# A hybrid mixer block: the gate logits of gated linear attention as a task of their own

## The chip, the cores and the metric

One core of one Trainium2 chip runs the whole block. The time is the device time of one execution in microseconds (us); of the kernel before, three runs gave 1382.53, 1382.78 and 1385.5, with the median 1382.78. Its five engines are TensorE (PE in the rows; PEld is its loading of weights), VectorE (DVE), ScalarE (ACT), GpSimd (POOL) and SyncE (SP, which issues most DMAs).

## The reference, cut to what matters

Two layers, each with four branches on the same normalised input: latent attention (MLA), neighbourhood attention, Hyena convolution, gated linear attention (GLA). There are 256 latent tokens and 256 context tokens; layer 0 gives out both streams, layer 1 only the latent one. The branches' outputs are gated, projected, weighted by merge gates and summed. What the change touches is the decay of GLA:

```python
def feats(hh):
    q, k = jnp.split(in_proj(hh, w_in, 'gla_qk').astype(f32), 2, axis=-1)
    ...
    glr = in_proj(hh, w_in, 'gla_glr').astype(f32).reshape(B, L, 2, GLA_GATE_RANK)
    logit = jnp.einsum('blir,ire->blie', glr, wg2.astype(f32)) + bg.astype(f32)
    log_a = (jax.nn.log_sigmoid(logit) / GLA_TAU).reshape(B, L, 2, GLA_HEADS, GLA_DK)
    return q, k, v, log_a

def gla_chunked(q, k, v, log_a, s0):
    ...
    b = jnp.cumsum(g, axis=3)          # g: log_a in chunks of 64 tokens
    a = jnp.einsum('nbhtd,nbhsd->nbhts', q * jnp.exp(b - b_mid), k * jnp.exp(b_mid - b))
    ...
```

The logarithm of the sigmoid is written as min(x, 0) - ln(1 + exp(-|x|)), where x is the logit with its bias. It is needed for all 512 tokens in two directions, 256 channels each: four tiles of 128 x 512 per layer.

## The kernel before, in words

Nearly all products are made of three passes (mm3): each operand is split into a rounded high part and a rest, and high x high, high x low and low x high are summed in PSUM. For weights, the method piece loads 512 KB into one of three raw buffers through SyncE's queue, ScalarE casts the high part (wh, line 439) and VectorE subtracts (wl, line 380). Names in the rows: pc and pj are projections by channel and by token, br the branch projection into the merged sum, sc the scores, pt the transposed probabilities, y the attention's output, lg the gate logits, ktp the transposed keys of GLA, kv, atp and go its state, score and output products, ot the transposes of its output.

The order of TensorE's instructions is written out by hand. Generators ("tasks") yield either a delay or a condition. The driver has a clock of its own, which each product moves on by a cost; it takes the first task by priority whose delay is over, and so lays out one fixed queue for TensorE. Priority 0 goes first (attention units, GLA's passes), then 1 (MLA, GLA), 2 (the adaLN weights), and 5, the main line with the projections, fills what is left. The delays stand in the table WAIT, a pair for each name, for layer 0 and layer 1. They only decide where on TensorE's queue a product stands; the hardware waits by semaphores. The order on the other engines is chosen by a planner from the program's order and modelled times, and tiles get free buffers of their pool there. Pools that matter: T (15 buffers of 128 x 512), S (20), G (8, which the merge gates and filters use), raw (3).

The main line of a layer: MLA's gate, then gla_in (queries, keys and values of GLA), while MLA runs as a task; the merge gates of branch 0, first half; a wait for MLA's end; branch 0's projection, first half; then the GLA task starts (method gla). Beside it run the second half of branch 0's merge gate and projection, GLA's gate gla_z, and both halves of the merge gate of branch 3; then the main line waits for GLA's end and projects it.

GLA itself first loads the logits' weights (raw, wg), splits them, makes the four logit tiles in PSUM (lg), and computes on VectorE mn = min(x, 0), ee = max(x, 0), ee = mn - ee, which is -|x|. ScalarE then takes Exp and Ln of the four tiles in this order (line 1196), and GpSimd subtracts. Then come two passes over pairs of heads, each with two directions (gla_dir): a scan over the decays on VectorE (line 1238), exponentials, the transposes ktp, the states, scores and outputs. The second pass starts when the first has ended. At last come a norm and the transposes ot.

Of the kernel before, what the change touches and what calls it, by code (L numbers as in the profile page):

```python
# [12 lines left out]
AF = mybir.ActivationFunctionType  # L13
ALU = mybir.AluOpType
# [111 lines left out]
def _layout(x, c, ctx, c_ctx, ada_w, ada_b, pre_g, post_g, w_in, mla_q_norm, mla_w_uq, mla_kv_norm, mla_w_ukv, na_rpb,  # L126
# [78 lines left out]


WAIT = {
    "ada_at0": (6.0, 8.0),
    "ada_at1": (6.0, 11.0),
    "ada_at2": (15.0, 17.0),  # L210
    "ada_at3": (17.5, 19.5),
# [3 lines left out]
    "norm": (4.23, 4.0),  # L215
    "norm_turn": (5.27, 5.25),
    "norm_ab": (0.16, 0.69),
    "norm_step": (1.25, 0.52),
    "filt_in": (3.1, 4.0),
    "filt_sin1": (6.0, 15.54),  # L220
    "filt_sin2": (6.0, 4.8),
# [2 lines left out]
    "filt_sum": (10.0, 11.8),  # L224
    "filt_norm": (7.2, 15.6),
    "filt_dft": (0.3, 0.5),
    "filt_out": (1.82, 4.9),
    "probs": (5.63, 6.08),
    "probs2": (7.2, 7.6),
    "probs_out": (1.36, 1.35),  # L230
    "values_out": (1.14, 5.3),
    "latent_in": (1.5, 1.5),
    "latents": (10.0, 12.0),
    "latents_out": (5.62, 0.49),
    "mla_keys": (1.6, 1.78),
    "mla_v": (0.32, 0.22),
    "mla_k": (0.8, 2.25),
    "mla_q": (0.08, 0.5),
    "mla_q_out": (1.7, 1.04),
    "na_in": (2.87, 0.97),  # L240
    "hy_turn": (2.18, 3.82),
    "hy_turn_step": (0.35, 0.5),
    "hy_turn_out": (0.5, 0.67),
    "hy_dft": (1.57, 1.8),
    "hy_product": (13.35, 11.95),
    "hy_mid": (0.35, 0.81),
    "hy_out_step": (0.72, 0.5),
    "hy_order": (6.38, 0.9),
    "hy_out": (1.3, 1.0),
    "gla_in": (2.65, 0.53),  # L250
    "gla_logit": (2.0, 0.1),
    "gla_decay": (7.1, 2.9),
    "gla_dir": (6.79, 4.0),
    "gla_norm": (14.0, 4.73),
    "gla_turn": (0.03, 0.45),
    "gla_out": (1.66, 1.98),
    "gla_keys": (6.49, 5.03),
    "gla_kT": (0.9, 1.07),
    "gla_at": (0.5, 0.5),
    "gla_scores": (6.1, 4.0),  # L260
    "gla_o": (2.0, 1.09),
    "merged": (4.6, 3.55),
    "merged_step": (0.48, 0),
    "merged_out": (1.6, 1.24),
    "norm_first": (3.27, 8.0),
}

# [6 lines left out]
class Block:  # L274
# [890 lines left out]
        v = yield from self.tok_values(l, "gla_v")  # L1165
        return q, k, v

    def gla(self, l, outs, qkv, g, ys):
        nc, d = self.nc, self.d
        q, k, v = qkv  # L1170
        lo = outs[0] * 256
        raw = self.T("wg2", (P, 2, 2, P))
        nc.gpsimd.dma_start(raw[:96], d["wg2"][l])
        wg = self.tp.tile([P, 2, 2, P], F32R, tag="t", name=self.name("wg"))
        nc.scalar.copy(wg[:96], raw[:96])
        self.sub(nc.vector, wg[32:64], raw[32:64], wg[32:64].bitcast(F32))
        yield self.wait("gla_in")
        la, es = {}, {}
        for p in range(2):
            for r in range(2):  # L1180
                ps = self.ps(self.pa, "lg")

                self.mm(ps, wg[:96, r, p, :], self.glrT[:96, :])
                mn, mx = self.S("mn"), self.T("ee")
                bg = self.pp(l, "bg", 2 * r + p)
                self.ts(mn, ps, bg, ALU.add, 0.0, ALU.min)
                self.ts(mx, ps, bg, ALU.add, 0.0, ALU.max)
                self.sub(nc.vector, mx, mn, mx)
                la[p, r], es[p, r] = mn, mx
                yield self.wait("gla_logit")  # L1190

        last = None
        for f, bias in ((AF.Exp, 0.0), (AF.Ln, 1.0)):
            for e in es.values():
                with self.tc.issue_after(last) if last is not None else nullcontext():
                    i = nc.scalar.activation(e, e, f, bias=bias)
                last = i.ins if hasattr(i, "ins") else i
        for key, e in es.items():
            self.sub(nc.gpsimd, la[key], la[key], e)
        yield self.wait("gla_decay")  # L1200
        o = [self.S("glao", (P, 4, P)) for _ in range(4)]
        for p in range(2):
            ts_ = []
            for r in range(2):
                ts_.append(self.spawn(self.gla_dir(p, r, outs, la[p, r], q[p], k[p], v, o), 0))
                yield self.wait("gla_dir")
            yield lambda: all(t.done for t in ts_)
        t0 = 2 * outs[0]
        nt = 4 - t0
        ss = []  # L1210
        for h in range(4):
            sq = self.T("osq", (P, 4, P))
            ss.append(self.t(4, "oss"))
            nc.scalar.activation(sq[:, t0:], o[h][:, t0:], AF.Square)
            nc.vector.tensor_reduce(out=ss[h][:, :nt], in_=sq[:, t0:], axis=AX.X, op=ALU.add)
        for h in range(4):
            rs = self.rstd(ss[h][:, :nt], nt, 1.0 / P)
            self.mul(nc.vector, o[h][:, t0:], o[h][:, t0:], rs.unsqueeze(2).to_broadcast([P, nt, P]))
        yield self.wait("gla_norm")
        yield lambda: g() is not None  # L1220
        for h in range(4):
            ps = self.ps(self.pt, "ot")
            for tt in range(t0, 4):
                self.tr(ps[:, tt * P : tt * P + P], o[h][:, tt, :])
            y = self.T("y32")
            self.stt(y[:, lo:], ps[:, lo:], self.pp(l, "gla_norm"), g()[h][:, lo:], ALU.mult, ALU.mult)
            self.split(ys[0][h][:, lo:], ys[1][h][:, lo:], y[:, lo:], nc.gpsimd)
            yield self.wait("gla_turn")
        yield self.wait("gla_out")
# [187 lines left out]
    def layer(self, l, ws):  # L1417
        nc, d = self.nc, self.d
        self.l = l
        outs = (0, 1) if l < DEPTH - 1 else (1,)  # L1420
# [5 lines left out]
        lats = []  # L1426
# [10 lines left out]
        gz = {}  # L1437
        ys = self.ytiles()
# [5 lines left out]
        mla = self.spawn(start_mla(), 1)  # L1444
        gz["mla"] = yield from self.zgate(l, "mla_z", outs, True)
        qkv = yield from self.gla_in(l, outs)
        if l == 0:
            self.rest = self.spawn(self.ada_rest(), 2)
        gates = yield from self.gate_list(l, 0, (0,), outs)
# [4 lines left out]
                merged[s, half] = self.M("merged")  # L1454
        box = {}
        yield from self.merge_list(l, 0, (0,), gates, ys, merged, True)
        gla = self.spawn(self.gla(l, outs, qkv, lambda: gz.get("gla"), box), 1)
        gates = yield from self.gate_list(l, 0, (1,), outs)
        yield from self.merge_list(l, 0, (1,), gates, ys, merged, True)
        ys = self.ytiles()  # L1460
# [126 lines left out]
```

## Time and profile before

| | us |
|---|---|
| median of the runs | 1382.78 |
| profiled execution, its own time | 1384.55 |
| its span, first to last instruction | 1382.8 |
| TensorE busy | 1311.0 |
| VectorE busy | 898.5 |
| ScalarE busy | 604.2 |
| GpSimd busy | 319.1 |

The profile comes from one execution. Busy times are of instructions that work, not of waits. A product's start and end are modelled, so products that follow one another overlap in the rows. In a row of waits, "PE ktp <- DVE ktl" is idle time of TensorE ahead of ktp that ended when VectorE had written ktl. The granted clock is a share of full speed, 2.4 GHz; at 0.5 TensorE runs at 1.2 GHz. "issue" means that no releaser shows.

### The profile page before, as it was taken

What the parts mean: (1) busy time and instruction counts of PE and PEld (TensorE: products, weight loads), DVE (VectorE), ACT (ScalarE), POOL (GpSimd) and SP (SyncE); (2) the same over time, 40 slices, a digit from 0 to 9 for tenths busy, and PEclk for the clock granted to TensorE, in tenths of its full rate; (3) what the DMA queues carried; (4) which work ended last, traced back from release to release, by engine and by line L of the source; (5) the groups of instructions that cost most, each with busy time, mean ns of one, the idle gap of its engine ahead of it and who ended that gap; (6) DMA issues with size and microseconds to landing.
All of it is one profiled execution on the core that took longest, in us unless ns stands there. A gap on an engine that the chain in (4) does not pass through costs nothing.

```text
span 1382.8 us, 20166 instructions
## 1 busy us (share of the span) xinstructions
PE 1311.0 (95%) x7444; PEld 1033.8 (75%) x7444; DVE 898.5 (65%) x1676; ACT 604.2 (44%) x1268; POOL 319.1 (23%) x408
## 2 busy tenths in 40 slices
PE   6999999989999999999999999989996999999997
PEld 3877677767877776766767777778775899788875
DVE  5678663675443446556566587887677787768763
ACT  4555553432323233222344543565546456444552
POOL 2332201243320101123201122442104331122110
PEclk9999999999999999999999999999998999999998
DMA  9521223332243433423422343433143366435361
GB/s 349 204 92 39 91 77 97 101 99 78 92 125 135 141 118 109 135 92 106 139 92 81 103 153 111 158 107 114 42 147 92 108 198 210 157 108 166 109 217 56
DMA packets 55506, 171.07 MB, mean 124 GB/s; under 512 B 7470, under 2 KB 10128, under 8 KB 55408
## 3 DMA queue, kind: packets, MB, share of 16 engines
q1 hardware_dynamic: 49056, 153.31, 33.6%
q0 software_dynamic: 5440, 16.16, 3.6%
q8 instruction: 59, 0.97, 0.3%
q10 hardware_dynamic: 912, 0.31, 0.1%
q14 instruction: 39, 0.32, 0.1%
HBM read 163.45 MB, written 6.31 MB: 123 GB/s over the span
## 4 chain that ended last, share of the span: by engine, by line
PE 42%; DVE 7%; issue 3%; ACT 2%; DMA 2%; POOL 1%; DVEq 0%; POOLq 0%; ACTq 0%
PE pc L390 12%; PE pj L390 11%; PE br L390 5%; PE wo L390 3%; PE sc L390 2%; PE y L390 2%; PE pt L404 2%; DVE wl L380 2%; PE pa L390 1%; PE yc L390 1%; ACT wh L439 1%; DMA raw<-in_w_out 1%; DMA raw<-in_w_in 1%; DVE ub L374 0%; DVE wr L380 0%
## 5 line engine op out<-in xcount | busy, mean ns | idle before, releaser
L380 DVE TENSOR_TENSOR wl<-raw,wh 128x512 fp32r<-128x512 f32 (+1 forms) x416 | 300.3, 744 | 178.1 <-ACT wh L439 175.8
L439 ACT CAST wh<-raw 128x512 fp32r<-128x512 f32 (+1 forms) x416 | 248.5, 618 | 273.1 <-DMA raw<-in_w_in 143.4
L390 PE MATMUL pc<-hh,wh 128*128 128x256 f32 (+1 forms) x688 | 242.4, 352 | 6.5 <-DVE xt L387 2.7
L390 PE MATMUL pc<-hh,wl 128*128 128x256 f32 (+1 forms) x688 | 231.4, 336 | 0.0
L390 PE MATMUL pc<-hl,wh 128*128 128x256 f32 (+1 forms) x688 | 230.9, 336 | 0.0
L390 PE MATMUL pj<-wh,hh 128*128 128x512 f32 x512 | 213.2, 416 | 2.8 <-ACT wh L439 1.8
L390 PE MATMUL pj<-wl,hh 128*128 128x512 f32 x512 | 200.4, 391 | 0.4 <-DVE wl L380 0.4
L390 PE MATMUL pj<-wh,hl 128*128 128x512 f32 x512 | 200.3, 391 | 0.0
L390 PEld LDWEIGHTS pc<-hh,wh 128*128 128x128 f32 x688 | 132.1, 192 | 32.1 <-issue 15.1
L390 PEld LDWEIGHTS pc<-hl,wh 128*128 128x128 f32 x688 | 132.2, 192 | 14.3 <-issue 2.6
L390 PEld LDWEIGHTS pc<-hh,wl 128*128 128x128 f32 x688 | 131.8, 192 | 13.6
L390 PEld LDWEIGHTS pj<-wh,hh 128*128 128x128 f32 x512 | 96.4, 188 | 33.1 <-issue 12.4
L390 PEld LDWEIGHTS pj<-wh,hl 128*128 128x128 f32 x512 | 96.2, 188 | 21.1
L390 PEld LDWEIGHTS pj<-wl,hh 128*128 128x128 f32 x512 | 96.6, 189 | 20.3 <-issue 2.6
L380 POOL TENSOR_TENSOR gl<-y,gh 128x256 fp32r<-128x256 f32 (+1 forms) x44 | 36.2, 829 | 295.0 <-ACT gh L422 295.0
L826 ACT ACTIVATE p<-sc,mx 128x512 f32<-128x512 f32 (+1 forms) x96 | 58.9, 615 | 59.4 <-DVE mx L824 56.2
L390 PE MATMUL br<-wh,gh 128*128 128x512 f32 x192 | 79.2, 412 | 4.8 <-DVE merged L383 2.8
L390 PE MATMUL br<-wl,gh 128*128 128x512 f32 x192 | 76.9, 400 | 0.0
L390 PE MATMUL br<-wh,gl 128*128 128x512 f32 x192 | 76.7, 399 | 0.1
L1340 ACT ACTIVATE gt<-pj 128x512 f32<-128x512 f32 x48 | 28.6, 596 | 91.0 <-PE pj L390 88.5
L824 DVE TENSOR_REDUCE mx<-sc 128x1 f32<-128x512 f32 (+1 forms) x96 | 55.0, 591 | 11.4 <-PE sc L390 10.5
L841 ACT COPY pt<-pt 128x256 f32<-128x256 f32 x96 | 34.2, 372 | 43.1 <-PE pt L404 42.1
(287 smaller groups left out, 2227.0 us busy)
## 6 DMA issues: line engine op xcount, KB each, us to landing
raw<-in_w_in SPq DMA_DIRECT2D x160, 512.0 KB, 3.6
adaw<-in_ada_w SPq DMA_DIRECT2D x36, 512.0 KB, 3.6
raw<-in_w_branch SPq DMA_DIRECT2D x32, 512.0 KB, 3.7
raw<-in_w_out SPq DMA_DIRECT2D x16, 512.0 KB, 4.3
adaw<-in_ada_w SPq DMA_DIRECT2D x24, 256.0 KB, 5.2
H<-filt POOLq DMA_DIRECT2D x16, 256.0 KB, 4.3
nab<-in_na_bias POOLq DMA_DIRECT2D x16, 256.0 KB, 3.1
raw<-in_w_in SPq DMA_DIRECT2D x8, 448.0 KB, 4.5
```

The lines of the kernel that those rows point to most:

```text
L380: eng.tensor_tensor(out=out, in0=a, in1=b, op=ALU.subtract)
L390: self.nc.tensor.matmul(out, lhsT, rhs, start=start, stop=stop, skip_group_check=skip)
L404: self.nc.tensor.transpose(out, in_, self.ident)
L439: nc.scalar.copy(hi, raw[:, sl])
L824: nc.vector.tensor_reduce(out=mx, in_=ps[h][:, :nk], axis=AX.X, op=ALU.max, negate=True)
L826: nc.scalar.activation(p[h][:, :nk], ps[h][:, :nk], AF.Exp, bias=mx, scale=1.0, accum_out=sm)
L841: nc.scalar.copy(pts[h][b // 2], pp[:, b : b + 2, :])
L1340: self.nc.scalar.activation(gates[s, t], ps, AF.Tanh, scale=0.5)
```

## The change

The first half of gla becomes a method and task of its own, gla_logits, which the layer starts with priority 1 as soon as gla_in has ended (and the four latent tasks, which make glrT, are done; they are by then). gla starts where it did, waits for that task on the driver's clock, and goes straight to its passes. In the logits' work, VectorE keeps the min; ScalarE writes the absolute value from PSUM with the bias added, and Exp takes the sign by its scale, so the max and the difference go. mn moves from pool S to pool G. Eighteen entries of WAIT change; those of the two stages here are shown.

```diff
-    "ada_at0": (6.0, 8.0),
+    "ada_at0": (3.68, 7.47),
-    "probs_out": (1.36, 1.35),
+    "probs_out": (1.36, 0.94),
-    "mla_v": (0.32, 0.22),
+    "mla_v": (0.32, 0),
-    "mla_q": (0.08, 0.5),
+    "mla_q": (0.15, 0),
-    "hy_turn": (2.18, 3.82),
+    "hy_turn": (1.49, 4.79),
-    "gla_in": (2.65, 0.53),
-    "gla_logit": (2.0, 0.1),
+    "gla_in": (2.65, 0.67),
+    "gla_logit": (1.02, 0.1),
-    "gla_dir": (6.79, 4.0),
+    "gla_dir": (6.31, 4.0),
-    "gla_scores": (6.1, 4.0),
-    "gla_o": (2.0, 1.09),
+    "gla_scores": (5.09, 7.57),
+    "gla_o": (2.0, 1.05),
...
-    def gla(self, l, outs, qkv, g, ys):
+    def gla_logits(self, l, lats, la):
+
         nc, d = self.nc, self.d
-        q, k, v = qkv
-        lo = outs[0] * 256
+        yield lambda: len(lats) == 4 and all(t.done for t in lats)
         raw = self.T("wg2", (P, 2, 2, P))
         nc.gpsimd.dma_start(raw[:96], d["wg2"][l])
...
-        la, es = {}, {}
+        es = {}
...
-                mn, mx = self.S("mn"), self.T("ee")
+                mn, ab = self.G("mn"), self.T("ee")
                 bg = self.pp(l, "bg", 2 * r + p)
+                nc.scalar.activation(ab, ps, AF.Abs, bias=bg)
                 self.ts(mn, ps, bg, ALU.add, 0.0, ALU.min)
-                self.ts(mx, ps, bg, ALU.add, 0.0, ALU.max)
-                self.sub(nc.vector, mx, mn, mx)
-                la[p, r], es[p, r] = mn, mx
+                la[p, r], es[p, r] = mn, ab
                 yield self.wait("gla_logit")
...
-        for f, bias in ((AF.Exp, 0.0), (AF.Ln, 1.0)):
+        for f, scale, bias in ((AF.Exp, -1.0, 0.0), (AF.Ln, 1.0, 1.0)):
...
+    def gla(self, l, outs, qkv, la, logits, g, ys):
+        nc = self.nc
+        q, k, v = qkv
+        lo = outs[0] * 256
+        yield lambda: logits.done
...
         qkv = yield from self.gla_in(l, outs)
+        la = {}
+        logits = self.spawn(self.gla_logits(l, lats, la), 1)
```

## Rows read from the trace of the kernel before

**Rows 1.** the page's first part: busy us, share of the span, instructions
```profile
PE 1311.0 (95%) x7444; PEld 1033.8 (75%) x7444; DVE 898.5 (65%) x1676; ACT 604.2 (44%) x1268; POOL 319.1 (23%) x408
```

**Rows 2.** stretches: us, busy us (count) PE, PEld, DVE, ACT, POOL, clock, DMA, GB/s
```profile
1008.00:1029.50 21.50, 21.39 (x108) 16.29 (x106) 12.72 (x24) 12.10 (x25) 1.77 (x3) 1.00 0.40 132
1029.50:1113.66 84.16, 71.53 (x566) 60.12 (x565) 67.26 (x132) 44.30 (x85) 33.11 (x54) 0.92 0.34 107
1043.60:1053.90 10.30, 0.00 (x0) 0.00 (x0) 5.64 (x6) 8.83 (x13) 7.74 (x7) 0.75 0.48 150
1053.90:1062.70 8.80, 7.83 (x58) 6.37 (x59) 6.24 (x13) 2.13 (x5) 1.60 (x5) 0.51 0.05 20
203.00:246.00 43.00, 43.00 (x222) 31.89 (x221) 19.41 (x41) 16.33 (x35) 3.51 (x6) 1.00 0.35 114
```

**Rows 3.** TensorE's waits, 1000 to 1130: total us, times, longest
```profile
PE ktp L404 <- DVE ktl L374: 10.3, 1, 10.3
```

**Rows 4.** timeline, layer 1's GLA: start us, us, instruction, idle before
```profile
1030.86 0.40 PE L390 MATMUL lg<-glrT,wg 96*128 96x512 f32 x1
1045.52 2.27 DVE L1238 TENSOR_TENSOR_SCAN gb<-scan_mask,mn 128x512 f32<-128x512 f32 x1 [1.98 <-POOL mn L380]
1053.92 1.11 PE L404 MATMUL ktp<-ident,ktl 128*128 128x128 f32 x4 [10.33 <-DVE ktl L374]
1058.54 1.82 PE L390 MATMUL kv<-gla_v,kT 64*64 64x128 f32 x20 [0.95 <-ACT kT L1263]
1110.52 0.38 PE L404 MATMUL ot<-ident,glao 128*128 128x128 f32 x2
```

**Rows 5.** timeline of ScalarE there, its table loads
```profile
1042.22 1.28 ACT L1196 ACT_TABLE_LOAD   x1
1045.20 1.28 ACT L1340 ACT_TABLE_LOAD   x1
1047.11 1.28 ACT L1196 ACT_TABLE_LOAD   x1
1050.08 1.28 ACT L1250 ACT_TABLE_LOAD   x1
```

**Rows 6.** tiles mn, ee, wg: ns min/median/max, first and last start
```profile
L387 DVE TENSOR_SCALAR mn<-lg,par x8: 739/746/752, 250.0 to 1036.7; 128x512 f32<-128x512 f32 x8
L387 DVE TENSOR_SCALAR ee<-lg,par x8: 739/740/743, 250.7 to 1037.4; 128x512 f32<-128x512 f32 x8
L380 DVE TENSOR_TENSOR ee<-mn,ee x8: 677/682/693, 251.5 to 1039.8; 128x512 f32<-128x512 f32 x8
L1196 ACT ACTIVATE ee<-ee x16: 612/630/634, 252.2 to 1048.4; 128x512 f32<-128x512 f32 x16
L380 POOL TENSOR_TENSOR mn<-mn,ee x8: 1262/1291/2179, 264.0 to 1049.1; 128x512 f32<-128x512 f32 x8
L1175 ACT CAST wg<-wg x2: 609/616/622, 227.5 to 1028.2; 96x512 fp32r<-96x512 f32 x2
DMA to landing us min/median/max: 2.7/2.8/2.9
```

**Rows 7.** timeline: issues of the logits' weights; MLA's last value product
```profile
212.53 0.54 POOL L1173 DMA_DIRECT2D wg<-in_wg  x1
1008.50 0.54 POOL L1173 DMA_DIRECT2D wg<-in_wg  x1
1021.32 1.95 PE L390 MATMUL y<-pt,mlav 128*64 128x256 f32 x16
```

**Rows 8.** TensorE's waits from 250 to 345, layer 0's GLA
```profile
PE ada L390 <- issue: 4.9, 2, 3.7
PE br L390 <- DVE merged L383: 2.8, 1, 2.8
PE ktp L404 <- DVE ut L383: 0.9, 1, 0.9
```

**Rows 9.** groups of ScalarE: busy, mean ns, idle before
```profile
L754 ACT ACTIVATE fabs<-filt 128x512 f32<-128x512 f32 x16 | 9.8, 627 | 7.3 <-DVE filt L374 7.2
```

More of the change, by code (lines that the diff above doesn't have):

```diff
@@ L217 @@
     "norm_ab": (0.16, 0.69),
-    "norm_step": (1.25, 0.52),
+    "norm_step": (0.65, 0.52),
     "filt_in": (3.1, 4.0),
@@ L226 @@
     "filt_dft": (0.3, 0.5),
-    "filt_out": (1.82, 4.9),
+    "filt_out": (1.82, 4.04),
     "probs": (5.63, 6.08),
-    "probs2": (7.2, 7.6),
-    "probs_out": (1.36, 1.35),
+    "probs2": (7.2, 7.7),
+    "probs_out": (1.36, 0.94),
     "values_out": (1.14, 5.3),
-    "latent_in": (1.5, 1.5),
+    "latent_in": (2.81, 1.5),
     "latents": (10.0, 12.0),
@@ L235 @@
     "mla_keys": (1.6, 1.78),
-    "mla_v": (0.32, 0.22),
+    "mla_v": (0.32, 0),
     "mla_k": (0.8, 2.25),
-    "mla_q": (0.08, 0.5),
+    "mla_q": (0.15, 0),
     "mla_q_out": (1.7, 1.04),
     "na_in": (2.87, 0.97),
-    "hy_turn": (2.18, 3.82),
+    "hy_turn": (1.49, 4.79),
     "hy_turn_step": (0.35, 0.5),
     "hy_turn_out": (0.5, 0.67),
-    "hy_dft": (1.57, 1.8),
-    "hy_product": (13.35, 11.95),
+    "hy_dft": (1.57, 2.98),
+    "hy_product": (12.59, 11.95),
     "hy_mid": (0.35, 0.81),
-    "hy_out_step": (0.72, 0.5),
+    "hy_out_step": (0.72, 0),
     "hy_order": (6.38, 0.9),
     "hy_out": (1.3, 1.0),
-    "gla_in": (2.65, 0.53),
-    "gla_logit": (2.0, 0.1),
+    "gla_in": (2.65, 0.67),
+    "gla_logit": (1.02, 0.1),
     "gla_decay": (7.1, 2.9),
-    "gla_dir": (6.79, 4.0),
+    "gla_dir": (6.31, 4.0),
     "gla_norm": (14.0, 4.73),
@@ L259 @@
     "gla_at": (0.5, 0.5),
-    "gla_scores": (6.1, 4.0),
-    "gla_o": (2.0, 1.09),
+    "gla_scores": (5.09, 7.57),
+    "gla_o": (2.0, 1.05),
     "merged": (4.6, 3.55),
     "merged_step": (0.48, 0),
-    "merged_out": (1.6, 1.24),
+    "merged_out": (0.82, 1.24),
     "norm_first": (3.27, 8.0),
@@ L1183, in gla @@
                 self.mm(ps, wg[:96, r, p, :], self.glrT[:96, :])
-                mn, mx = self.S("mn"), self.T("ee")
+                mn, ab = self.G("mn"), self.T("ee")
                 bg = self.pp(l, "bg", 2 * r + p)
+                nc.scalar.activation(ab, ps, AF.Abs, bias=bg)
                 self.ts(mn, ps, bg, ALU.add, 0.0, ALU.min)
-                self.ts(mx, ps, bg, ALU.add, 0.0, ALU.max)
-                self.sub(nc.vector, mx, mn, mx)
-                la[p, r], es[p, r] = mn, mx
+                la[p, r], es[p, r] = mn, ab
                 yield self.wait("gla_logit")
         last = None
-        for f, bias in ((AF.Exp, 0.0), (AF.Ln, 1.0)):
+        for f, scale, bias in ((AF.Exp, -1.0, 0.0), (AF.Ln, 1.0, 1.0)):
             for e in es.values():
                 with self.tc.issue_after(last) if last is not None else nullcontext():
-                    i = nc.scalar.activation(e, e, f, bias=bias)
+                    i = nc.scalar.activation(e, e, f, scale=scale, bias=bias)
                 last = i.ins if hasattr(i, "ins") else i
@@ L1456, in layer @@
         yield from self.merge_list(l, 0, (0,), gates, ys, merged, True)
-        gla = self.spawn(self.gla(l, outs, qkv, lambda: gz.get("gla"), box), 1)
+        gla = self.spawn(self.gla(l, outs, qkv, la, logits, lambda: gz.get("gla"), box), 1)
         gates = yield from self.gate_list(l, 0, (1,), outs)
```

## The prediction

> **What bounds the kernel now.** Start with the page's busy times: TensorE is busy for 95% of the span [rows 1]. All that an edit elsewhere can win is TensorE's idle time, 1382.8 - 1311.0 = 71.8 us, and time that it spent at the lower clock after idling. So the second view is the table of stretches, read for TensorE's busy time and granted clock. The worst place is in layer 1, at the start of the gated linear attention (GLA). In the 10.30 us from 1043.60 TensorE does nothing, and in the 8.80 us after that it is granted 0.51 of full speed, that is, the lower level, 1.2 GHz [rows 2]. Third, the waits of that stretch name the reason: one wait of 10.3 us of the first key transposes, ktp, for VectorE's ktl [rows 3]; the timeline adds one of 0.95 us of the products kv for ScalarE's kT [rows 4].
>
> The timeline says why ktl is late. The first gate logit product runs at 1030.86, the first scan only at 1045.52, and ktp at 1053.92 [rows 4]. Between lie VectorE's min, max and difference for four tiles, ScalarE's Exp and Ln with table loads, and GpSimd's subtraction. ScalarE changed its table four times in these 9 us, at 1.28 us each, because the gates' Tanh fell between the logarithms [rows 5]. The products that could have covered this, a merge gate and part of a branch projection, lasted the 14.1 us from 1029.5 and had run out at 1043.6. Layer 0 has twice the tokens, hence twice the cover: there TensorE's waits hold no ktp for a ktl [rows 8].
>
> **The change part by part.** The logits and logarithms become a task that starts when the values of GLA are projected, beside the last units of the latent attention (MLA); the GLA task then begins with the scan.
>
> *Removed, layer 1.* The two waits are 10.33 + 0.95 us [rows 4]. After them TensorE was busy 7.83 us at the half clock [rows 2]; at 2.4 GHz this work takes half, so 3.9 us more come back if no long gap stands before it. Together 15.2 us. The four logit products only move, at no gain.
>
> Is something else late next? From the first scan to the last output transpose the old chain takes 1110.52 - 1045.52 = 65.0 us [rows 4], with the old waiting list. If the scan starts where the stage starts, at 1029.5, this chain ends at 1094.5. TensorE's own work needs 84.16 - 15.2 = 69.0 us [rows 2], to 1098.5. TensorE stays the bound, by 4 us. The new list lengthens gla_scores from 4.0 to 7.57 in layer 1, for two passes that follow one another: at most 7.1 us more on the chain, 3 us past TensorE. I take 0 here, since a wait in that list places work on TensorE's queue and need not idle it while other products are there; 3 us goes to the range.
>
> *Added beside MLA, layer 1.* The stage from the last GLA value to the start of GLA is 1008.0 to 1029.5, 21.5 us, with ScalarE busy 12.10 and VectorE 12.72 [rows 2]. VectorE's twelve instructions (4 x 0.746 + 4 x 0.740 + 4 x 0.682 = 8.7 us) shrink to four mins, 3.0 us [rows 6]: 15.7 of 21.5, covered. ScalarE gets four absolute values at about 0.63 [rows 9] (that row reads SBUF without a bias tile; the upper bound is VectorE's 0.746 for the same tile from PSUM, 0.5 us more for four), without a load for the function, since what L754 waited for is VectorE, plus eight Exp and Ln at 0.63 [rows 6], and at least two table loads, 2.6 us: 12.1 + 2.5 + 5.0 + 2.6 = 22.2 us in 21.5. ScalarE is full there, and its queue also carries the softmax, the casts of the weights and the gates. What waits behind a late logarithm is the softmax or a weight cast, and TensorE waits for those. MLA's last value product follows the gate's last product by hardly a gap at 1021.32 [rows 7], so that tail has little to spare. From below: 0, since some of ScalarE's work may slide into the stage after, where it is busy for only 44.30 of 84.16 us [rows 2]. From above: were every Ln cut off from the next by an Exp or Tanh, eight loads, 10.3 us, give 29.9 us, 8.4 over. I take 2, near the two-load case, which the order written into the code (all Exp, then all Ln) favours. GpSimd's four subtractions, 1.29 each [rows 6], find it idle but for 1.77 us [rows 2]; up to one of them may stand ahead of the last split of y: within the 2.
>
> ScalarE's table is where a rule bears on this. Four loads in 9 us stand in the trace, the last of them between a logarithm and an Exp [rows 5]. "ScalarE: Activation LUTs" of the Trainium skill, section "Table sets: the hidden batching unit", asks for calls to be batched by set, and the change puts Ln among the softmax's Exps, which speaks against it. The same section says that one set holds both exp and ln, so that an Exp behind an Ln would be free; the load at 1050.08 disagrees, and the measurement decides. By the Trainium skill's set ScalarE's sum would be 20.9 instead of 22.2 us, and the price nearer 0 than 2.
>
> *The weights of the logits.* Their load, cast and split move to the start of the new task. The load takes 2.8 us, the cast 0.62, the difference about 0.68 [rows 6]: 4.1 us. The first logit product now stands 0.67 us behind the last value projection in layer 1 and 2.65 us in layer 0, at the head of TensorE's in-order queue. In the trace the loads were issued at 1008.50 and 212.53 [rows 7], some 20 us ahead of their casts, so GpSimd does run ahead of TensorE's place in the program. If the issue doesn't move, the product waits until 1012.6 in layer 1 (3.9 us) and 216.6 in layer 0, where its place is about 205.7 (10.9 us). If it moves as far ahead as before, it waits for nothing. I take 1 us per layer, near the lower end, since both loads led so far. The mins' new pool is that of the gates, 8 buffers; a gate list takes four in layer 0 and two in layer 1, so with the four mins the pool holds until the gates of GLA, by when the first pass's scans have freed two: no price.
>
> *Layer 0.* ScalarE is busy 16.33 of 43 us between the last value and the start of GLA [rows 2], so the logits fit. Its stalls afterwards (2.8 for a merge, 4.9 without a releaser, 0.9 [rows 8]) aren't caused by the logits: between -8.6 and 0 is the gain; I take 0.
>
> *The waiting list.* 18 entries change, most by under 1.5 us in one layer. Outside the places priced so far they move the order on TensorE's queue. I can't price them singly; recorded waits of that kind are 0.9 to 2.8 us each [rows 3, 8], so I give ±3 and take 0.
>
> Sum: -15.2 + 2 + 1 + 1 = -11.2 us. The profiled execution took 1384.55, so it would take 1373.4; that execution is 1.8 above the median of the runs, and from the median 1382.78 the forecast is 1371.6.
>
> **The rivals.**
>
> *ScalarE's jam.* The Ln are torn apart by Exp and Tanh; the price in layer 1 is 8.4 instead of 2, with 2 us of logit waits as before: 1382.8 - 15.2 + 8.4 + 2 = 1378. For it: the old stage did just that, four loads [rows 5]. The batching rule of the Trainium skill's page cited above points the same way. Against: most of the 48 gate products stand between, and ScalarE may catch up. Chance 0.13.
>
> *The chain becomes the bound.* The 3 us above, and a scan that is late by what the logarithms lack: from the first product to the first scan it took 14.7 us; from 1008.7 this ends at 1023.4, 6 us early, and with 22.2 us of ScalarE work in 21.5 about 2 us late. 1371.6 + 3 + 2 = 1377. Against: the same 6 us. Chance 0.12.
>
> *Slower: the logit products wait at the head of TensorE's queue.* The load of the weights finds no free buffer of the 15 that MLA's tiles share, or no turn on GpSimd, before the old issue times. 10.9 us in layer 0 and 3.9 in layer 1, and the lower clock after each: 3.9 us after a gap of 10 as measured, about half after the shorter. 10.9 + 3.9 + 3.9 + 2 = 20.7 against 15.2: 5.5 slower, 1388. It decides from the point where these waits with their clock pass 15.2. For it: MLA uses most of those buffers, and the change holds six of them at the worst time. Against: GpSimd idled long before both loads, and a load comes earlier in the program now. Chance 0.09.
>
> *More than said.* Layer 0's stalls of 8.6 us vanish as their cause, late VectorE work, is thinned by 5.7 us per layer: 1371.6 - 8.6 = 1363. Chance 0.11.
>
> **How the numbers follow.** The forecast has 0.55, with a range of its own from 1367 to 1377 (3 either way for the list, and the prices, 4 in all, between 2 and 6). Below it 0.11, above it 0.12 + 0.13, beyond the old time 0.09. A measurement of this kernel tells about 0.2%, 2.8 us. Faster by more: all but the slower rival and the worst ends of the jam, 0.86; within: 0.06; slower: 0.08. The range 1364 to 1381 leaves out the slower rival and the far end of the good one, some 0.15.
>
> **What would show it.** Right: in layer 1 ktp waits less than 1 us for ktl, the granted clock stays at full speed through the GLA stage, which shrinks from 84 to about 69 us; the products lg stand before MLA's last value product; VectorE shows 8 instructions for mn and none for ee. The price shows as waits of lg for wg, or of y, br or pt for ScalarE, between 1000 and 1030, and as more than two table loads per layer there. The prediction is wrong if ktp still waits for 5 us or more, if lg waits over 5 us in a layer, or if TensorE idles before the merge of GLA for its last transposes.

## The result, and the profile after

The changed kernel took 1362.0 us (median of 4 runs, 1359.06 to 1362.93), the kernel before 1384.14 in the runs beside it: a ratio over all runs of 0.9832, 95% interval 0.9804 to 0.986. That is 22 us faster, twice the forecast of 11, and below the predicted range of 1364 to 1381. The profiled execution took 1361.8, its span is 1360.0.

The page of the changed kernel, first part (columns as in [rows 1]):

```profile
PE 1305.9 (96%) x7444; PEld 1028.4 (76%) x7444; DVE 887.8 (65%) x1660; ACT 604.5 (44%) x1274; POOL 317.6 (23%) x408
```

TensorE's idle time falls from 71.8 to 54.1 us, its busy time from 1311.0 to 1305.9 with the same 7444 products, so some of them ran at a higher clock. VectorE has the sixteen instructions less that the diff takes away; ScalarE is no less busy.

To see where the 22.8 us of span went, both traces are cut where TensorE's main line begins the same group of products. In order, the four rows are layer 0's gated linear attention (GLA, from the second half of branch 0's merge gate to branch 3's projection), layer 0's Hyena (from there to branch 2's projection), layer 1's latent attention (MLA, to branch 0's projection), and layer 1's GLA (from there to branch 3's projection). Columns as in [rows 2]; first the kernel before:

```profile
245.50:389.60 144.10, 135.49 (x959) 105.78 (x958) 81.51 (x144) 49.77 (x87) 45.38 (x71) 0.98 0.29 91
389.60:649.10 259.50, 251.84 (x1185) 189.55 (x1183) 139.52 (x223) 74.61 (x128) 45.58 (x43) 0.99 0.36 117
906.50:1023.20 116.70, 113.14 (x704) 94.16 (x703) 83.34 (x165) 68.38 (x157) 25.93 (x28) 1.00 0.31 100
1023.20:1113.50 90.30, 77.57 (x591) 64.42 (x589) 70.50 (x137) 47.35 (x91) 33.68 (x55) 0.92 0.35 111
```

The same stretches of the changed kernel:

```profile
246.30:379.30 133.00, 130.92 (x955) 102.74 (x954) 64.47 (x124) 39.61 (x71) 38.10 (x61) 1.00 0.31 101
379.30:629.60 250.30, 247.66 (x1185) 187.40 (x1183) 139.40 (x221) 74.14 (x129) 44.91 (x42) 1.00 0.37 122
887.50:1009.50 122.00, 117.46 (x708) 96.47 (x706) 87.08 (x166) 74.33 (x167) 30.39 (x32) 0.99 0.27 86
1009.50:1087.60 78.10, 74.66 (x585) 62.23 (x586) 64.35 (x129) 40.75 (x83) 28.00 (x52) 0.98 0.45 140
```

The reader is to see two things. Layer 1, where the forecast put its whole gain, gives 12.2 us in the GLA stretch and pays 5.3 of it back in the MLA stretch; its Hyena stretch, not shown, grows by 2.6 (128.6 to 131.2). Net, layer 1 gives about 4; the rest of the kernel lengthens by some 2 in all. Layer 0, where the forecast had nothing, gives 11.1 in GLA and 9.2 in Hyena. Of these 20.3 us, 11.6 are idle time of TensorE that is gone (stretch less PE busy: 8.6 to 2.1, and 7.7 to 2.6). The other 8.7 are busy time, with the granted clock up from 0.98 and 0.99 to 1.00; 0.9 of it is the four logit products (0.23 each), which now stand ahead of the GLA stretch.

Layer 1, TensorE's longest waits of the changed kernel from 985 to 1088 (what waited for what: total us, times, longest):

```profile
PE br L390 <- DVE wl L380: 1.6, 2, 0.9
PE ktp L404 <- DVE ut L383: 1.3, 2, 0.9
PE lg L390 <- DVE wg L380: 0.7, 1, 0.7
```

The 10.3 us wait of [rows 3] is gone, and nothing of its size stands in its place. Layer 1's GLA stretch falls into two parts, branch 0's projection (first half) and the stage that the forecast cut out, from the second half of the merge gate on. Before, the parts took 6.3 us (1023.20 to 1029.50) and the 84.16 of [rows 2]; in the changed kernel:

```profile
1009.48:1018.82 9.34, 7.75 (x24) 5.71 (x25) 8.22 (x11) 5.90 (x13) 4.12 (x5) 0.82 0.49 164
1018.82:1087.74 68.92, 67.06 (x562) 56.69 (x561) 56.30 (x119) 34.87 (x72) 23.90 (x47) 1.00 0.45 137
```

So the stage is 15.2 us shorter and runs at the full clock, and the projection ahead of it is 3.0 longer, at 0.82. ScalarE's timeline of the changed kernel there (start us, us, instruction), with its table loads:

```profile
1003.52 1.28 ACT L1195 ACT_TABLE_LOAD   x1
1004.82 2.20 ACT L1195 ACTIVATE ee<-ee 128x512 f32<-128x512 f32 x4
1007.03 1.28 ACT L1345 ACT_TABLE_LOAD   x1
1008.32 0.60 ACT L1345 ACTIVATE gt<-pj 128x512 f32<-128x512 f32 x1
1008.82 3.21 ACT L439 CAST wh<-raw 128x512 fp32r<-128x512 f32 x6
```

Two loads, not the four of [rows 5]: the four Ln run in one piece. The price is in the last line: the weight casts stand behind Ln, load and Tanh and begin at 1008.82, VectorE's wl follow them, and br waits twice for wl, 1.6 us in all.

Tiles of the changed kernel (ns min/median/max, first and last start):

```profile
L1186 ACT ACTIVATE ee<-lg,par x8: 672/689/702, 206.1 to 1002.0; 128x512 f32<-128x512 f32 x8
L387 DVE TENSOR_SCALAR mn<-lg,par x8: 743/750/751, 206.8 to 1002.7; 128x512 f32<-128x512 f32 x8
```

Layer 0, TensorE's waits of the changed kernel from 246 to 380:

```profile
PE ktp L404 <- DVE ut L383: 1.5, 1, 1.5
PE adat L390 <- DVE ut L383: 0.3, 1, 0.3
PE ot L404 <- DVE y L383: 0.2, 1, 0.2
```

These three answer to [rows 8]: the waits of ada without a releaser (4.9) and of br for merged (2.8) are gone. So the question for the experiments is what these had to do with the gate logits.

### The profile page after: what moved, and what is told of

Its sections match the earlier page's. It is cut to its first block, busy times and chain, and to the rows that moved or that the text cites. A ratio compares the mean times of both kernels' runs of the same rounds, so it can differ in the third digit from the quotient of the medians.

```text
span 1360.0 us, 20150 instructions
## 1 busy us (share of the span) xinstructions
PE 1305.9 (96%) x7444; PEld 1028.4 (76%) x7444; DVE 887.8 (65%) x1660; ACT 604.5 (44%) x1274; POOL 317.6 (23%) x408
## 5 line engine op out<-in xcount | busy, mean ns | idle before, releaser
L390 PE MATMUL pc<-hh,wh 128*128 128x256 f32 (+1 forms) x688 | 239.6, 348 | 3.6 <-DVE xt L387 2.7
L390 PEld LDWEIGHTS pc<-hh,wh 128*128 128x128 f32 x688 | 131.1, 191 | 27.4 <-issue 13.9
L377 POOL TENSOR_TENSOR merged<-merged,gt 128x512 f32<-128x512 f32 x24 | 33.2, 1387 | 83.1 <-DVE gt L383 83.1
```

The lines of the kernel that those rows point to most:

```text
L377: eng.tensor_tensor(out=out, in0=a, in1=b, op=ALU.add)
L390: self.nc.tensor.matmul(out, lhsT, rhs, start=start, stop=stop, skip_group_check=skip)
```

## The experiments

"Old" is a value of the kernel before, "new" one of the changed kernel. Lengths are those of the stretches above. Each time is a median; its ratio is to the kernel before on the same chip, over all runs, so not exactly that of the medians. The kernel before took 1382.95 to 1384.74 beside these runs, so medians of different experiments are compared to within some 2 us.

**The two halves of the change.** First the moved task with the old list, then the new list on the old code.

```diff
 # the changed kernel, e1_old_list
-    (18 new entries of WAIT)
+    (the 18 old ones)
```

> The changed kernel with all 18 entries of the waiting list set back: the task and the absolute value alone. Theory A (the moved logits alone make the gain, in both layers): the stretch of layer 0's GLA, 144.1 us before and 133.0 changed, is about 133, and the time is within 4 us of the changed kernel's 1362. Theory B (the list made the gains in layer 0): that stretch stays near 144 and layer 0's Hyena stretch near 200 (200.8 before, 191.0 changed); only layer 1's GLA gains its 12 us less some 5 beside the latent attention, so about 1377.

1380.44 us, 0.9979 [0.9966, 0.9993]. The code alone is worth some 3 us. Its MLA and GLA stretches of layer 1:

```profile
902.50:1034.60 132.10, 122.17 (x708) 100.33 (x706) 86.92 (x168) 79.97 (x173) 30.95 (x32) 0.94 0.27 86
1034.60:1109.00 74.40, 72.58 (x585) 61.35 (x585) 61.19 (x125) 37.45 (x78) 27.74 (x51) 1.00 0.42 138
```

GLA gives 15.9 us, but the MLA stretch grows by 15.4. Its waits from 1000 to 1036, and ScalarE's table loads:

```profile
PE lg L390 <- DVE wg L380: 3.3, 1, 3.3
PE y L390 <- ACT pt L841: 2.7, 1, 2.7
```

```profile
1021.22 1.28 ACT L1195 ACT_TABLE_LOAD   x1
...
1024.20 1.28 ACT L1345 ACT_TABLE_LOAD   x1
...
1026.11 1.28 ACT L1195 ACT_TABLE_LOAD   x1
...
1031.43 1.28 ACT L1345 ACT_TABLE_LOAD   x1
```

Here ScalarE's jam and the late logit weights, two of the rivals, did happen, with the clock at 0.94 in that stretch: with the old list the task carries layer 1's hole from one stage to the one before. In layer 0 the code alone does move something: Hyena falls from 259.5 to 251.9, with every entry of the old list in place. GLA stays at 143.1; the waits of [rows 8] give way to another, which the kernel before doesn't have:

```profile
PE adat L390 <- DVE ut L383: 6.3, 1, 6.3
```

```diff
 # the kernel before, e2_new_list
-    (18 old entries of WAIT)
+    (the 18 new ones)
```

> The kernel before with the 18 new entries, logits in their old place on VectorE. Theory A: no better than 1380, and ktp still waits some 10 us for ktl in layer 1. Theory B: layer 0's two stretches gain their 21 us without the task, so about 1365, with ktp's wait still there.

1392.25, 1.0061 [1.0042, 1.008]: 8.5 us slower. Layer 0's GLA takes 146.6 and its Hyena 257.6, layer 1's MLA 119.8 and Hyena 131.5. Code alone -3, list alone +8.5, together -22: the gain lies in neither half.

**Which entries.** Groups of entries of the changed kernel were put back to the old values.

```diff
 # the changed kernel, e4_gla_old
-    "gla_in": (2.65, 0.67),
-    "gla_logit": (1.02, 0.1),
-    "gla_dir": (6.31, 4.0),
-    "gla_scores": (5.09, 7.57),
-    "gla_o": (2.0, 1.05),
+    (the old pairs)
```

> The changed kernel with the five entries of GLA set back (gla_in, gla_logit, gla_dir, gla_scores, gla_o). If the old delays, set for a stage that began with the logits, cause layer 0's stalls, its GLA stretch returns from 133.0 to about 143 us; layer 1's shrinks from 78 to about 75, as with the whole old list; together about 1369. Rival: layer 0's gain doesn't hang on them, 133 and about 1359.

1380.43, 0.9972 [0.996, 0.9983]. Layer 0's GLA is back at 142.3 and its Hyena at 258.6; layer 1 is as in the changed kernel (123.5, 77.2). GLA's entries carry 18 us, and those in layer 0. The longer gla_scores of layer 1 changes nothing there.

```diff
 # the changed kernel, e10_gla0_old: layer 0 alone
-    "gla_logit": (1.02, 0.1), "gla_dir": (6.31, 4.0), "gla_scores": (5.09, 7.57),
+    "gla_logit": (2.0, 0.1), "gla_dir": (6.79, 4.0), "gla_scores": (6.1, 7.57),
```

> The changed kernel with only layer 0's halves of three GLA entries set back: gla_logit 2.0, gla_dir 6.79, gla_scores 6.1. Theory: these decide where layer 0's second pass meets the transposes of the adaLN pieces; the stretch of layer 0's GLA goes from 133.0 to about 142 us, with a wait of adat for ut of some 6 us, and layer 1 stays at 122 and 78. Time about 1372 to 1378. Rival: layer 1's entries reach back through the planner, and layer 0 stays at 133.

1380.4, 0.9983 [0.9969, 0.9998]: three numbers make the 18 us. GLA 142.8, Hyena 260.4. TensorE's waits in its layer 0 GLA:

```profile
PE adat L390 <- DVE ut L383: 6.3, 1, 6.3
PE kv L390 <- ACT kT L1268: 1.6, 1, 1.6
PE ada L390 <- issue: 1.3, 1, 1.3
```

The product adat finishes a piece of the adaLN coefficients. It has nothing to do with GLA's states ut, but it takes its PSUM bank from the same pool of two that ktp and kv use (pt in the code), and a bank of kv is free only when VectorE has run through the states. VectorE's work in this stretch is less than before (68.2 us busy against 81.5), and still the stretch takes 142.8.

```diff
 # the changed kernel, e16_scores0_old, and e17_dir0_old
-    "gla_scores": (5.09, 7.57),
+    "gla_scores": (6.1, 7.57),
...
-    "gla_dir": (6.31, 4.0),
+    "gla_dir": (6.79, 4.0),
```

> The changed kernel with one delay of layer 0 as before, gla_scores 6.1. The three old delays together cost 18 us. Theory: what decides is where the adaLN transposes fall against the key transposes and state products of GLA, which gla_dir sets; in this kernel the first of them stands behind the scores as in the changed kernel, so nearly all is kept, 1362 to 1366. Rival: gla_scores, the largest of the three changes (1.0 in each of two passes), carries the loss: 1375 to 1380, with adaLN's transposes waiting some 6 us.

> The changed kernel with one delay of layer 0 as before, gla_dir 6.79. Theory: with it an adaLN transpose falls between the key transposes and the state products of the second direction, as in the kernel with all three old delays; so it brings the wait of about 6 us for a PSUM bank back, GLA's stretch of layer 0 goes from 133 to about 142, the Hyena stretch to 258, and the time to 1375 to 1380. Rival: the loss needs all three, or gla_scores: 1362 to 1366.

1378.91, 0.9958 [0.994, 0.9976], and 1378.01, 0.9955 [0.9935, 0.9976]; GLA takes 144.6 in both, as before the change, and Hyena 254.0 and 254.6, less than the 258 expected. The first run refutes the theory as I put it: gla_dir isn't the one that decides. The second bears out the mechanism. Each delay alone brings nearly the whole loss, and they don't add: in both an adat stands where the banks are held. TensorE and VectorE in the second pass of e17_dir0_old:

```profile
294.44 1.15 PE L390 MATMUL kv<-gla_v,kT 64*64 64x128 f32 x24
...
299.93 1.70 DVE L383 SCALAR_TENSOR_TENSOR ut<-ut,ff,kv 128x128 f32<-128x128 f32 x4
...
301.32 1.01 PE L390 MATMUL adat<-rows,par 128*2 128x256 f32 x2 [5.05 <-DVE ut L383]
```

And the same pass in the changed kernel:

```profile
289.77 0.49 PE L390 MATMUL kv<-gla_v,kT 64*64 64x128 f32 x10
...
295.46 0.63 PE L404 MATMUL ktp<-ident,ktl 128*128 128x128 f32 x4 [1.46 <-DVE ut L383]
...
297.40 1.04 PE L390 MATMUL kv<-gla_v,kT 64*64 64x128 f32 x22
...
302.57 0.59 PE L390 MATMUL adat<-rows,par 128*2 128x256 f32 x2 [0.34 <-DVE ut L383]
```

In the first an adat comes straight behind kv and TensorE stands still until the states are done; in the second other products stand there, and adat comes 4 us after the second kv. In e16_scores0_old it waits too, in the first pass, but other waits together are longer:

```profile
PE adat L390 <- DVE ut L383: 3.0, 1, 3.0
PE kv L390 <- DVE gb L377: 2.3, 1, 2.3
PE kv L390 <- ACT kT L1268: 1.9, 2, 1.7
```

So there the bank is a part of the loss; no run gives its share.

**The remedy at the bank.** If that is the mechanism, another pool for adat must cure the old delays.

```diff
 # e4_gla_old, e11_gla_old_bank
-        ps = self.ps(self.pt, "adat")
+        ps = self.ps(self.pa, "adat")
```

> The changed kernel with the five old GLA entries, where adat waited 6.2 us in layer 0, and adat's PSUM tile taken from the pool of four banks instead of the pool of two that kv fills. Theory: that wait is for a bank which VectorE's chain ut still reads, so it goes to under 1 us and layer 0's GLA stretch falls from 142.3 to about 134 to 136 with the clock that comes back. Rival: adat waits for something else, or the next ktp takes over the same wait, and the stretch stays at 140 or more.

1370.14, 0.9913 [0.9888, 0.9938], against 1380.43 without it. The wait of adat is gone, GLA takes 139.0 and Hyena 255.1. What is left:

```profile
PE ada L390 <- issue: 2.2, 1, 2.2
PE ktp L404 <- DVE ut L383: 2.2, 1, 2.2
```

TensorE's order of products is the same as in e4_gla_old, and that on the other engines differs only in places, so the bank was worth about half of the 18 us. The transposes ktp, which still use the pool of two, wait.

```diff
 # the changed kernel, e12_bank
-        ps = self.ps(self.pt, "adat")
+        ps = self.ps(self.pa, "adat")
```

> The changed kernel with adat's PSUM tile from the pool of four banks. In it adat waited only 0.3 us, so if its gain in layer 0 is that adat no longer meets the two full banks, this adds nothing: layer 0's GLA stretch 132 to 134, the time 1360 to 1364. If the banks still cost it something, as the 1.5 us of ktp suggest, it gains up to 3 us and beats the changed kernel. Rival: the pool of four then makes the attention's products wait, and it is slower by 2 us or more.

1365.89, 0.9873 [0.9848, 0.9897]: no gain; a loss shows in the stretch (138.7 instead of 133.0), while the intervals of the times overlap. TensorE's order is again the same. Without a fault to cure, adat now waits in the other pool, which GLA's scores and outputs use (3.7 and 1.6 us for VectorE's at).

**The ada products without a releaser.** In the kernel before, SyncE's queue and TensorE:

```profile
295.18 0.33 SPq L552 DMA_DIRECT2D adaw<-in_ada_w  x1
...
300.14 0.64 PE L390 MATMUL ada<-adaw,sv 128*32 128x256 f32 x8 [3.67 <-issue]
```

The product stands still behind a load issued 5 us earlier, which landed 3.6 us after its issue, as such loads do here (3.4 to 3.6); the last 1.4 us of the wait have no releaser in the trace. SyncE didn't issue it earlier because it waited itself, for another weights' load to land and then for VectorE:

```profile
SPq L552 <- DMA raw<-in_w_in: 3.1, 1, 3.1
SPq L552 <- DVE ut L1282: 2.3, 1, 2.3
```

The adaLN weights take the same three raw buffers as the other weights, in the same queue. A longer delay between load and product should cure it, and it is one number:

```diff
 # the kernel before, e13_ada_later
-    "ada_load": (7.75, 9.57),
+    "ada_load": (9.5, 9.57),
```

> The kernel before with the adaLN pieces of layer 0 standing 1.75 us further behind their loads (ada_load 9.5 instead of 7.75), nothing else. Theory: the 4.9 us that TensorE waited without a releaser in layer 0 are adaLN products whose load landed late; they go or shrink below 2, and since all later pieces shift too, the stretches of layer 0 change by several us: GLA's from 144.1 to about 138, time 1375 to 1381. Rival: those waits have another cause, the stretch stays at 144 and the time at 1384.

1376.03, 0.9956 [0.9936, 0.9977]; GLA of layer 0 from 144.1 to 137.0. Its longest wait there:

```profile
PE br L390 <- ACT gt L1340: 2.7, 1, 2.7
```

So the stalls of [rows 8] that the forecast left at 0 were worth 7 us of this stretch, and go without touching GLA. Of layer 0's other stretches, Hyena gains 3.4 and the neighbourhood attention loses 7.0 (152.2 to 159.2), so the time shows 7 us, not more.

```diff
 # the changed kernel, e14_after_ada_later
-    "ada_load": (7.75, 9.57),
+    "ada_load": (9.5, 9.57),
```

> The changed kernel with layer 0's adaLN pieces 1.75 us further behind their loads, as tried on the kernel before. Theory: the 20 us won in layer 0 are a matter of where the adaLN pieces fall among GLA's and Hyena's products; the new list fits the old spacing, so moving them all breaks the fit: layer 0's GLA and Hyena stretches grow by 5 us or more together (133.0 and 250.3), the time is 1366 to 1378. Rival: the gain is a property of the earlier logits and stays: the two stretches within 3 us, the time within 4 of 1362.

1373.93, 0.9922 [0.99, 0.9943]: 12 us worse than the changed kernel. GLA and Hyena nearly keep their gain (386.5 together, 383.3 in the changed kernel), against the theory, but the adaLN pieces now run on into the neighbourhood attention, and the rest of layer 0 goes from 257.9 to 269.4, with TensorE's waits there:

```profile
PE pt L404 <- DVE pt L839: 2.9, 1, 2.9
PE sc L390 <- ACT p L826: 2.7, 1, 2.7
```

**One layer alone.**

```diff
 # the changed kernel, e9_layer1_only
+        if l == 0: (the task starts where gla starts, as in the kernel before)
```

> The changed kernel with the task started early in layer 1 only; in layer 0 it starts where GLA starts, as before. Theory: layer 0's GLA stretch needs both the moved logits and the list, so it returns from 133.0 to 143 to 147 us and the time to about 1374. Rival: layer 0 hangs on the list alone, 133 and 1362.

1379.52, 0.9966 [0.9955, 0.9978]. Layer 1 is that of the changed kernel (122.1, 78.1), layer 0's GLA takes 148.1: the new delays fit only with the logits moved. The early task in layer 0 is worth 17.5 us of the time, though no product waited for the logits. What stands there instead is a wait at the same two banks:

```profile
PE ktp L404 <- DVE ut L383: 6.3, 2, 3.2
```

**MLA's entries and Hyena's.**

```diff
 # the changed kernel, e8_mla_old
-    "probs2": (7.2, 7.7), "probs_out": (1.36, 0.94), "mla_v": (0.32, 0), "mla_q": (0.15, 0),
+    "probs2": (7.2, 7.6), "probs_out": (1.36, 1.35), "mla_v": (0.32, 0.22), "mla_q": (0.08, 0.5),
```

> The changed kernel with the entries of the latent attention set back (probs2, probs_out, mla_v, mla_q). Theory: the shorter entries end the latent attention some 8 us ahead of the merge gate that fills TensorE's queue, so that ScalarE's logarithms delay nothing; without them layer 1's latent stretch goes from 122.0 us to 130 or more (132.1 with the whole old list), with about four table loads and waits of lg and y of some 3 us each, and the time to about 1371. Rival: another entry did it, the stretch stays at 122 and the time near 1362.

1367.42, 0.9876 [0.9848, 0.9905]. Layer 1's MLA takes 129.4 instead of 121.9, with the waits of the old list again:

```profile
PE y L390 <- ACT pt L841: 3.6, 1, 3.6
PE lg L390 <- DVE wg L380: 2.2, 1, 2.2
```

These entries end MLA earlier: its last value product runs at 999.57 in the changed kernel, 10 us ahead of the first product of br, where before hardly 2 us lay between [rows 7]. The logarithms then fall behind the softmax, not among it.

```diff
 # the changed kernel, e3_hyena_old; and the reverse on the kernel before, e7_hyena_new
-    "hy_turn": (1.49, 4.79), "hy_dft": (1.57, 2.98), "hy_product": (12.59, 11.95), "hy_out_step": (0.72, 0),
+    "hy_turn": (2.18, 3.82), "hy_dft": (1.57, 1.8), "hy_product": (13.35, 11.95), "hy_out_step": (0.72, 0.5),
```

> The changed kernel with the four Hyena entries set back (hy_turn, hy_dft, hy_product, hy_out_step). If these made the gain of layer 0's Hyena stretch, that stretch returns from 191 to about 200 us and the time goes to 1370 to 1372. If that gain came from elsewhere (what the planner made of the other engines' order), the stretch stays near 191 and the time within 3 us of 1362.

> The kernel before with the four Hyena entries of the new list alone. If these entries make the gain of layer 0's Hyena stretch by themselves, it falls from 259.5 us (with its leading products) to about 251 and the time to about 1376. If they fit only a stage that begins earlier against the adaLN pieces, the stretch stays within 3 us of 259.5 and the time within 4 of 1384.

1366.96, 0.9883 [0.9866, 0.99], and 1383.89, 1.001 [0.9998, 1.0022]. On the changed kernel the old entries cost 5.5 us in layer 0's Hyena (255.8), another 3.9 ahead of layer 0's GLA stretch and 3.1 behind Hyena, and give 2.2 back in layer 1's Hyena (129.0). On the kernel before, the new ones give 4.2 in layer 0 (255.3) and cost 2.5 in layer 1 (131.1), and nothing measurable is left. So the halves for layer 1 should be put back alone:

```diff
 # the changed kernel, e15_hyena1_old
-    "hy_turn": (1.49, 4.79), "hy_dft": (1.57, 2.98), "hy_out_step": (0.72, 0),
+    "hy_turn": (1.49, 3.82), "hy_dft": (1.57, 1.8), "hy_out_step": (0.72, 0.5),
```

> The changed kernel with the layer-1 halves of three Hyena entries of the waiting list as before (hy_turn 3.82, hy_dft 1.8, hy_out_step 0.5). Theory: the stretch of layer 1's Hyena took 131.2 us in the changed kernel and 131.0 to 131.5 in every run with the new entries, 128.6 to 129.0 in every run with the old ones, so they cost some 2.5 us whatever else is changed; here it comes to about 129 and the time to about 1359.5, below both kernels. Rival: what is gained there is lost in the stretch behind it (106.1 before), or layer 0 is given another order by it, and the time stays at 1362 or above.

1359.93, 0.9823 [0.9797, 0.9848]. The stretch takes 128.6 as before, layer 0 keeps its times (132.8, 250.5). It is the fastest median of all; against the changed kernel's 0.9832 [0.9804, 0.986] the intervals overlap, so the gain is shown in the stretch, not in the time.

**The absolute value.** On VectorE in the changed kernel, and alone in the kernel before.

```diff
 # the changed kernel, e5_vector_abs
-                nc.scalar.activation(ab, ps, AF.Abs, bias=bg)
+                self.ts(ab, ps, bg, ALU.add, 0.0, ALU.max)
+                self.sub(nc.vector, ab, ab, mn)
```

> The changed kernel with the maximum and the difference back on VectorE, in the new task; ScalarE takes no absolute value. Theory: VectorE's 5.7 us more per layer are covered beside the latent attention and ScalarE has 2.8 us less, so 1360 to 1365. Rival: the softmax's VectorE work is held up, each layer's latent stretch grows by 3 us or more, and the time is 1368 or above.

1364.91, 0.9856 [0.9839, 0.9873]. Layer 0's GLA stays at 132.1, layer 1's takes 81.0 instead of 78.1. About 3 us, with overlapping intervals, and none of it in layer 0.

```diff
 # the kernel before, e6_abs_only
-                self.ts(mx, ps, bg, ALU.add, 0.0, ALU.max)
-                self.sub(nc.vector, mx, mn, mx)
+                nc.scalar.activation(mx, ps, AF.Abs, bias=bg)
```

> The kernel before with only the absolute value on ScalarE: no task, old list. If VectorE's chain sets layer 1's ktl, eight instructions fewer (5.7 us) shorten ktp's wait from 10.3 to about 5 and the time falls by 5 to 8 us with its clock, to about 1377. If ScalarE's chain of tables and logarithms sets it, the four absolute values only lengthen that, ktp's wait stays at 10 or more and the time at 1384 or above.

1382.55, 0.9986 [0.9972, 1.0001], not to be told from nothing. Layer 0's GLA, with 5 us less of VectorE's work and TensorE's order unchanged, stays at 143.3. The wait of [rows 3] shrinks by 7 us, but others come, and the stretch only goes from 90.3 to 87.9:

```profile
PE ktp L404 <- DVE ktl L374: 3.4, 1, 3.4
PE kv L390 <- ACT kT L1262: 2.2, 1, 2.2
```

## Why the prediction was wrong

**Layer 1's hole, -15.2: right in mechanism and in size.** The stage that the forecast cut out went from 84.16 to 68.92 us at a clock of 1.00; it had said 69. With the old list it took 69.0 (e1). Of the 15.2, 0.9 is the logit products, which moved.

**The price beside MLA, 2 + 1: too small.** The MLA stretch grew by 5.3 and branch 0's projection, which the forecast counted to the same stage, by 3.0: 8.3 in place of 3. In it are the 0.9 of the logit products, which "only move", their wait of 0.7, the 1.6 of br for wl, and the lower clock behind these (0.82 in the projection). A weight cast behind a late logarithm was named in the forecast; its size was missed. The list alone makes the MLA stretch 3.1 longer and the projection 0.9 shorter (e2), so if the parts add, some 6 belong to the moved work. ScalarE shows the two loads that were reckoned with, but only because the list clears its way: without MLA's entries the price in the MLA stretch is 12.7 (e8), with the whole old list 15.4 (e1). The list, taken at 0 with "±3", decided this. The rule of the Trainium skill on batching by table set ("ScalarE: Activation LUTs", section "Table sets: the hidden batching unit") spoke against the change; 15.4 with four loads and 5.3 with two agree with it, though the order of the products differs too.

**Layer 0: the step that failed.** "Its stalls afterwards ... aren't caused by the logits: between -8.6 and 0 is the gain; I take 0", and with it "±3" for the list. Layer 0 gave 20.3 us. With it the sum closes: -15.2 + 8.3 + 2.6 (layer 1's Hyena) + some 2 elsewhere - 20.3 is the -22.8 of the span. The runs show what stood there instead: 18 us hang on three delays (e10), and the new delays give them only with the task moved (e9; the list alone leaves the two stretches at 404.2 together, 403.6 before). On TensorE's fixed queue an adaLN product that comes while kv holds both banks of a shared pool waits 3 to 6 us for VectorE's states (e10, e16, e17); a weight product whose load went out late waits 4 (the kernel before, e13); the new order has neither. Two terms were missed: the busy time at a lower clock that goes with each stall (4.6 in GLA, less 0.9 for the logit products), which was counted in layer 1 and left out of layer 0, and the next stretch, Hyena, 9.2.

**The rival "more than said" had the time, 1363, for a wrong reason.** It put the stalls down to VectorE's work. With that work given back (e5) layer 0's GLA stays at 132.1; with it taken out of the kernel before, TensorE's order unchanged (e6), at 143.3; and with the logits moved out of the stretch altogether (e10) it takes 142.8.

**The other rivals.** The jam and the waiting logit products came true only with old entries; the 8.3 is near the jam's 8.4, but with two loads, not four or eight. The chain didn't become the bound: gla_scores at 7.57 or 4.0 leaves layer 1's GLA at 78.1 or 77.2. No product waited for the logits' weights beyond 0.7 us (layer 1) in the changed kernel; the list alone was slower, but with the logits in their old place.

**Open.** Why layer 0's Hyena gains 9.2. The Hyena entries make some 5 of it in the changed kernel and 4 in the kernel before (e3, e7), but the code alone makes 7.6 with none of them (e1), so the parts don't add; and it loses with GLA's delays (260.4 in e10). TensorE's order of groups in that stretch is the same in the changed kernel, e5 and e15 (250.3 to 252.2). But e11 has the order of e10 and takes 255.1, and e17 has nearly that order and takes 254.6, so order on TensorE alone doesn't settle it. The order on the other engines was not tried singly. Nor is it shown which of the new delays removes which stall of [rows 8].

## What to carry to other kernels

In a queue that is laid out by hand, look at every small product of another task (here the adaLN transposes) and ask whose PSUM bank and whose DMA queue it needs: one in the wrong place stalled the whole engine here for 3 to 6 us, with a lower clock in the stretch (0.96 to 0.98 instead of 1.00). Moving work and retuning delays are one change: measured apart they gave -3 and +8.5, together -22. So stalls of a few us in a stretch that the edit "doesn't touch" belong in the range with their clock and their next stage, when the edit also moves the delays there.

## What the runs showed of the hardware

- The absolute value with a bias by tile from PSUM took 0.689 us for 128x512 on ScalarE, against 0.627 from SBUF without one [rows 9] and 0.750 for the min on VectorE. No table load stands with it: the two loads of layer 1's stage are those around Ln.
- A table load took 1.28 us each time, from Ln to Tanh as from the other functions to Ln.
- Two delays in the table that orders TensorE's queue, changed by 0.5 and by 1.0 us, moved the time by 16 and 17 us, each alone (e17, e16); three together by 18 (e10).
- With TensorE's order unchanged, the pool of PSUM banks of one small product moved the time by 10 us one way (e4 to e11) and its stretch by 5.7 us the other way (133.0 to 138.7, e12).
